# A two-block transformer kernel: norm factors spread by transposition, and wider products in the last up projection

## The chip, the core and the metric

The kernel runs on one core of a Trainium2 chip. The core has five engines that run side by side, each through its own queue in order: TensorE (PE: matrix products, with PEld for the load of the stationary operand), VectorE (DVE), ScalarE (ACT), GpSimd (POOL) and SyncE (SP, which starts the DMAs here). The metric is the time of one execution on the device in microseconds (us).

## What is computed

`reference.py` chains two layers over 256 positions of width 1024, in fp32. Cut to the parts that matter here:

```python
# first block
h = rmsnorm(x, g_mix);  z = h @ w_in            # gated conv branches, then
x = x + (g_a * y_a + g_b * y_b) @ w_o
u = rmsnorm(x, g_ffn) @ w_up                    # 1024 -> 2 x 2816
f = gelu(causal_dwconv(u[:, :D_FF]) + b) * u[:, D_FF:]
x = x + f @ w_down
x = x + sigmoid(rmsnorm(x, g_ple) @ w_ple_gate) * (p @ w_ple)
x = rmsnorm(x, g_final)
# second block
proj = rms_norm(x, attn_pre_g) @ w_in_2         # 8 window heads, 4 differential heads
x = x + rms_norm(mix @ w_out_2, attn_post_g)    # the "post-norm" below
u = rms_norm(x, ffn_pre_g) @ w_up_2             # 1024 -> 2 x 4096
c = causal_dwconv3(u, conv_w) + conv_b
x = x + rms_norm((gelu(c[:, :4096]) * c[:, 4096:]) @ w_down_2, ffn_post_g)
```

## The kernel before

Activations lie feature first: a tile is 128 features by 256 positions. Each fp32 operand of a product is split into a high part in the rounded format fp32r and the remainder, and a product `w x` becomes `wh xh + wh xl + wl xh`. Weights come in 128x128 blocks, eight to a group: SP loads a group (`raw`), ACT casts it to `hi`, DVE (in some stretches POOL) subtracts to get `lo`. An activation's two parts lie next to each other in one tile (`cr`).

There are two ways to run a block. `run` (line 463) issues three products of 256 columns: `wh xh`, `wh xl`, `wl xh`, all into one half of a PSUM bank, so a bank holds two output tiles. `run2` issues, for each group of eight blocks, eight products of 512 columns (`wh` against both parts at once, into a whole bank), then eight of 256 (`wl xh`); the two halves of the bank are added when it is read. So an output tile takes a whole bank. `w_o`, `w_down` and, from tile 4 on, `w_up` use `run2`; `w_up_2` uses `run` throughout.

An RMS norm is applied late where it can be: the products run on `x * g`, and the factor `1/rms` is multiplied in when the bank is read (`evac_pair`). Factors come from `norm_task`: a sum of squares, `s.mean` (products with a column of ones, one output column), `rstd` (DVE adds epsilon, POOL takes the power -0.5), then `spread_mm`, which copies the 2x128 factors over 128 partitions by a product of a broadcast column with the identity. `spread_mm` is called for 13 norms. `normed_task` makes operands that already hold the factor (`hn2` for `w_up`).

All instructions are recorded through `Plan`, whose cost table keeps a clock for each engine. A task is a generator; when it yields a list of tiles, `Plan.spawn` puts it on a heap with the time at which these are expected, and it goes on when TensorE's planned time has reached that. So the plan sets where, among the weight products, a norm's products stand in TensorE's queue. A task that yields "dve" goes on when the plan sees DVE idle.

At the end of attention stands the post-norm: four squares on ACT, sums on DVE, `mean` products, `rstd`, `spread_mm`, and then `x5_task` builds the new x and the operands of `w_up_2`, one of eight at a time. In between, `warm(n)` issues n transposes of the identity into an unused bank. The first four tiles of `w_up_2` then run with k outermost; after them, for each j from 4 to 31, two tiles of `w_up_2` (16 blocks) and, from j = 6 on, eight blocks of `w_down_2`, which accumulate in four banks.

Of the kernel before, what the change touches and what calls it, by code (L numbers as in the profile page):

```python
# [17 lines left out]
P = 128  # L18
T = 256
# [21 lines left out]


QA_PERM = [h * 64 + d for c in range(4) for h in (c, c + 4) for d in range(64)]
LAG2, OLD1, DOWN1, NGAP, PLU, POOL_END2 = 6, 4, 2, 0.9, (30, 8), 1


def _blocks(name, ms, ks):
# [118 lines left out]
    return [(name, i) for i in range(lo // T, hi // T + 1)]  # L166


class Plan:


# [38 lines left out]
    def spawn(self, gen):  # L210
        try:
            y = next(gen)
        except StopIteration:
            return
        if callable(y):
            self.waiting.append((y, gen))
        elif isinstance(y, str):
            self.fill[y].append(gen)
        else:
            self.n += 1  # L220
            at = self.now + y if isinstance(y, (int, float)) else self.at(y) - 0.15
# [116 lines left out]
def block_kernel(ctx: ExitStack, tc: tile.TileContext, w, xT, pT, vec, dist, gpost, out):  # L338
# [43 lines left out]
    def cf():  # L382
        return ap.tile([P, T], F32, tag="c", name=nm("cf"), bufs=NC)
# [27 lines left out]

    names = {}
    EARLY, LAST2 = 4, 4
    WARMA, WARMB = 8, 14
    POOL_END = 4
    POOL_LO, PL1, PL2, LIVE = 8, 0, 0, 4

# [187 lines left out]
    def spread_mm(q, r2):  # L605

        for h in range(2):
            TE.matmul(
                q[:, h * P : (h + 1) * P], lhsT=r2[:, h : h + 1].to_broadcast([P, P]), rhs=ident,
                start=True, stop=True,  # L610
            )

    def norm_task(s, d, box, keep=True, bank=None):

        yield s.done
        yield [s.acc]
        q = Bank()
        s.mean(q, d)
        yield [q.t]
        r = rstd(q[:, :2], 2)  # L620
        yield [r]
        spread_mm(q[:, T:], r)
        if keep:
            yield [q.t]
            o = cf()
            S.copy(o, q[:, T:])
            box[0] = o
            if bank is not None:
# [196 lines left out]
    def ln_task():  # L825
        yield lambda: lastconv[0]
        s = Sum(4, V)
        for c in range(4):
            s.add(acc[c])
        yield [s.acc]  # L830
        q = Bank()
        TE.matmul(q[:, :T], lhsT=ones512, rhs=s.acc, start=True, stop=True)
        yield [q.t]
        sv = Sum(4, V)
        ts = []
        for c in range(4):
            V.tensor_tensor(acc[c], acc[c], q[:, :T], op=ALU.subtract)
            t = cf()
            S.activation(t, acc[c], AF.Square)
            ts.append(t)  # L840
        for t in ts:
            sv.add(t)
        preload(AF.Silu)
        rl = [None]
        plan.spawn(norm_task(sv, 512, rl, False))
        yield lambda: rl[0] is not None
        yield [rl[0]]
        for c in range(4):
# [89 lines left out]
        S.activation(hl[:, 0, :], n, AF.Identity, scale=vec1(g, j))  # L938
        plan.spawn(lo_scaled(n, hl, vec1(g, j), h, j, s))

    def normed_task(r, g, h):

        yield lambda: r[0] is not None
        yield [r[0]]
        for j in range(8):
            t = cf()
            V.scalar_tensor_tensor(t, x[j], vec1(g, j), r[0], op0=ALU.mult, op1=ALU.mult)
            plan.spawn(split_task2(t, h, j))
            yield NGAP
# [191 lines left out]
    def r45_task():  # L1141
        yield lambda: n45[0] == 8
        q = q45
        ms = q[:, :4].rearrange("p (b i) -> p i b", i=2)
        yield [q.t]
        r4 = rstd(ms[:, 0, :], 2)
        yield [r4]
        t = small(2)
        V.tensor_tensor(t, ms[:, 1, :], r4, op=ALU.mult)
        V.tensor_tensor(t, t, r4, op=ALU.mult)  # L1150
        r5 = rstd(t, 2)
        spread_mm(q[:, T:], r4)
# [300 lines left out]
    xt = [[None, None], [None, None]]  # L1453
    gp = []
    og = []
    acc6 = None
    for p in range(4):
        sq = ap.tile([P, 512], F32, tag="pair", name=nm("pT"), bufs=NPAIR)
        S.activation(sq, ob[p].t, AF.Square)
        t = cf()  # L1460
        V.tensor_tensor(t, sq[:, :T], sq[:, T:], op=ALU.add)
        if p in (1, 2):
            V.tensor_tensor(t, t, acc6, op=ALU.add)
        last6, acc6 = acc6, t
    q6 = Bank()
    for n, a in enumerate((last6, acc6)):
        for h in range(2):
            mmul(q6[:, h : h + 1], a[:, h * P : (h + 1) * P], means[DM], q6.first(), n == 1)
    for p in range(4):
        u = pair()  # L1470
        for i in range(2):
# [36 lines left out]

    plan.spawn(x5_task())
    del ob, odst  # L1510
    f, ups = [None] * 32, [0, 0]

    def f2_task(j, q):
        yield lambda: r7[0] is not None
        yield [q.t, r7[0]]
        yield lambda: ups[0] - ups[1] < 4
        u = evac_pair(q, r7[0])
        ups[0] += 1
        del q
# [12 lines left out]
        hl = parts()  # L1532
        S.copy(hl[:, 0, :], c)
        yield [hl]
        V.tensor_tensor(hl[:, 1, :], c, hl[:, 0, :].bitcast(F32), op=ALU.subtract)
        f[j] = hl

    ffn_first("w_up_2", 4, 32, h7, f2_task)
    plan.spawn(xt_task())
    down = [[Bank() for _ in range(2)] for _ in range(2)]  # L1540

    def run_half(tt, k, wh, wl, fp, banks=(0, 1)):
        plan.work(plan.at((wh, wl, fp)))
        a, b = (fp[:, i, tt * P : (tt + 1) * P] for i in range(2))
        for i in banks:
            o = down[tt][i].t
            cs = slice(i * 512, (i + 1) * 512)
            mmul(o, a, wh[:, cs], k == 0, False)
            mmul(o, a, wl[:, cs], False, False)
            mmul(o, b, wh[:, cs], False, k == 31)  # L1550
# [43 lines left out]
        D.dma_start(out=t, in_=gpost[:, i * 512 : (i + 1) * 512])  # L1594
        gp.append(t)
    for j in range(4, 32):
        plan.until(lambda: ups[0] > j - 4)
        q = Bank()
        run(("w_up_2", j), {j: (q, 0), 32 + j: (q, 1)}, h7, 7)
        plan.spawn(f2_task(j, q))  # L1600
        del q
        if j >= LAG2:
            run_down(j - LAG2)
    for k in range(32 - LAG2, 32 - LAST2):
# [68 lines left out]
```

## Time and profile before

| | us |
|---|---|
| median of 3 runs (lowest, highest) | 776.12 (775.79, 776.43) |
| profiled execution | 775.53 |
| its span in the profile | 773.7 |
| busy: PE, DVE, ACT, POOL | 757.9, 627.5, 451.6, 91.0 |

The span is what the profile shows of the execution; some 1.8 us lie around it. PE is busy in 98% of the span. A row of PE gives a start, a length, the product's output and operands, and in brackets the idle time before it and what ended that.

### The profile page before, as it was taken

What the parts mean: (1) busy time and instruction counts of PE and PEld (TensorE: products, weight loads), DVE (VectorE), ACT (ScalarE), POOL (GpSimd) and SP (SyncE); (2) the same over time, 40 slices, a digit from 0 to 9 for tenths busy, and PEclk for the clock granted to TensorE, in tenths of its full rate; (3) what the DMA queues carried; (4) which work ended last, traced back from release to release, by engine and by line L of the source; (5) the groups of instructions that cost most, each with busy time, mean ns of one, the idle gap of its engine ahead of it and who ended that gap; (6) DMA issues with size and microseconds to landing.
All of it is one profiled execution on the core that took longest, in us unless ns stands there. A gap on an engine that the chain in (4) does not pass through costs nothing.

```text
span 773.7 us, 14017 instructions
## 1 busy us (share of the span) xinstructions
PE 757.9 (98%) x5364; PEld 708.6 (92%) x5364; DVE 627.5 (81%) x1149; ACT 451.6 (58%) x797; POOL 91.0 (12%) x75
## 2 busy tenths in 40 slices
PE   7999999999999999999999999999999999999996
PEld 7999999999888888889988899999999999999995
DVE  5699978898988886756879896889978787777883
ACT  7575466566766664545738554757655555555551
POOL 2589200022000000111000010220000000000000
PEclk9999999999999999999999999999999999999999
DMA  8656637454665556555335345354655555555531
GB/s 302 224 183 218 195 135 235 159 178 138 219 199 199 185 180 215 166 201 178 99 94 196 105 149 159 103 191 136 219 193 188 181 182 193 180 191 186 196 110 54
DMA packets 39667, 135.69 MB, mean 175 GB/s; under 512 B 4528, under 2 KB 6320, under 8 KB 39600
## 3 DMA queue, kind: packets, MB, share of 16 engines
q1 hardware_dynamic: 39600, 134.80, 53.0%
q8 instruction: 42, 0.69, 0.4%
q14 instruction: 25, 0.20, 0.1%
HBM read 133.73 MB, written 1.05 MB: 174 GB/s over the span
## 4 chain that ended last, share of the span: by engine, by line
PE 92%; DVE 2%; issue 2%; POOL 1%; DMA 1%; ACT 1%; SPq 0%; POOLq 0%; DVEq 0%; ACTq 0%
PE ps L289 92%; DMA pair<-xT_in 1%; POOL cf L289 1%; DVE cf L289 1%; SPq L289 0%; POOL small L289 0%; DVE lo L289 0%; ACT hi L289 0%; ACT pT L289 0%; ACT cf L289 0%; DVE pT L289 0%; DVE small L289 0%; DVE pair L289 0%; ACT cr L289 0%; POOLq L1668 0%
## 5 line engine op out<-in xcount | busy, mean ns | idle before, releaser
L289 PE MATMUL ps<-cr,hi 128*128 128x256 f32 (+1 forms) x2880 | 568.9, 305 | 4.3 <-ACT hi L289 4.3
L289 PEld LDWEIGHTS ps<-cr,hi 128*128 128x128 f32 x2880 | 462.8, 192 | 23.7 <-ACT hi L289 4.3
L289 PE MATMUL ps<-cr,lo 128*128 128x256 f32 x1704 | 411.3, 283 | 0.3 <-DVE lo L289 0.3
L289 DVE TENSOR_TENSOR lo<-raw,hi 128x1024 fp32r<-128x1024 f32 (+2 forms) x237 | 284.5, 1214 | 40.9 <-ACT hi L289 39.9
L289 PEld LDWEIGHTS ps<-cr,lo 128*128 128x128 f32 x1704 | 301.8, 192 | 8.2 <-DVE lo L289 0.7
L289 ACT CAST hi<-raw 128x1024 fp32r<-128x1024 f32 (+2 forms) x255 | 258.1, 1028 | 36.6 <-PE ps L289 18.3
L289 PE MATMUL ps<-hi,cr 128*128 128x512 f32 (+2 forms) x320 | 98.2, 375 | 0.0
L289 DVE SCALAR_TENSOR_TENSOR cf<-pair,vt,cf 128x254 f32<-128x254 f32 (+2 forms) x144 | 66.4, 481 | 19.8 <-ACT cf L289 17.3
L289 DVE SCALAR_TENSOR_TENSOR cf<-ps,vt,cf 128x255 f32<-128x255 f32 (+30 forms) x172 | 69.2, 458 | 5.4 <-ACT cf L289 4.6
L289 PEld LDWEIGHTS ps<-hi,cr 128*128 128x128 f32 x320 | 58.9, 188 | 10.5 <-issue 0.7
L289 ACT ACTIVATE cf<-pair,vt 128x256 f32<-128x256 f32 x68 | 37.5, 599 | 49.6 <-DVE pair L289 49.6
L289 POOL TENSOR_TENSOR small<-small,mh 128x2 f32<-128x2 f32 (+1 forms) x15 | 14.5, 968 | 407.0 <-DVE small L289 399.0
L289 POOL TENSOR_TENSOR cf<-cf,cf 128x256 f32<-128x256 f32 x28 | 31.1, 1110 | 260.4 <-ACT cf L289 250.0
L289 PE MATMUL ps<-lo,cr 128*128 128x512 f32 (+2 forms) x160 | 60.0, 375 | 0.0
L289 ACT CAST cr<-cf 128x256 fp32r<-128x256 f32 x66 | 26.5, 407 | 55.2 <-DVE cf L289 55.1
L289 POOL TENSOR_TENSOR lo<-raw,hi 128x1024 fp32r<-128x1024 f32 x18 | 42.9, 2416 | 10.0 <-ACT hi L289 8.4
L289 ACT ACTIVATE cf<-cf 128x256 f32<-128x256 f32 x62 | 25.2, 416 | 23.7 <-DVE cf L289 23.6
L289 DVE TENSOR_TENSOR pair<-ps,cf 128x512 f32<-128x512 f32 (+1 forms) x58 | 35.5, 615 | 3.1 <-ACT cf L289 1.9
L289 ACT ACTIVATE cr<-pair,vt 128x256 fp32r<-128x256 f32 x24 | 12.2, 510 | 43.5 <-DVE pair L289 43.5
L289 DVE TENSOR_TENSOR cr<-cf,cr 128x256 fp32r<-128x256 f32 x64 | 26.2, 420 | 11.8 <-ACT cr L289 11.7
L289 PEld LDWEIGHTS ps<-lo,cr 128*128 128x128 f32 x160 | 30.2, 189 | 4.0
L289 ACT COPY cf<-ps 128x256 f32<-128x256 f32 x50 | 18.3, 367 | 23.8 <-PE ps L289 23.7
(104 smaller groups left out, 385.0 us busy)
## 6 DMA issues: line engine op xcount, KB each, us to landing
raw<-w_in SPq DMA_DIRECT2D x244, 512.0 KB, 4.0
raw<-w_in SPq DMA_DIRECT2D x8, 320.0 KB, 2.9
pair<-xT_in SPq DMA_DIRECT2D x8, 128.0 KB, 5.6
out<-pT SPq DMA_DIRECT2D x3, 256.0 KB, 2.1
pair<-gpost_in SPq DMA_DIRECT2D x2, 256.0 KB, 4.9
vt<-vec_in SPq DMA_DIRECT2D x1, 420.5 KB, 6.1
dt<-dist_in SPq DMA_DIRECT2D x1, 384.0 KB, 7.2
raw<-w_in SPq DMA_DIRECT2D x2, 128.0 KB, 2.2
```

Of the source, the lines that this page charges most:

```text
L289: r = f(*args, **kw)
```

## The change

Four things are changed. (1) `spread_mm` uses TensorE's transpose in place of a product with the identity. (2) In the post-norm the last pair's squares are no longer added up on DVE: both halves go to `mean` products of their own (eight such calls in place of four); seven `warm` transposes now stand ahead of the means, and seven in place of fourteen behind the spread. (3) A norm task that yields `Late([...])` goes on 0.6 us later in the plan's time. (4) From j = 15 on, `w_up_2` runs with `run2` on operands `hn7` that already hold the factor; `hn7` is made by `normed_task` in DVE's idle time, and each of the two tiles of a j gets its own bank, read by the new `f2b_task`. The four banks of `w_down_2` are taken when first used. In `w_up` the tile 4 goes from `run2` to `run` (OLD1 from 4 to 5).

```diff
+LATE = 0.6
+OLD2, WAIT2 = 15, 2
-LAG2, OLD1, DOWN1, NGAP, PLU, POOL_END2 = 6, 4, 2, 0.9, (30, 8), 1
+LAG2, OLD1, DOWN1, NGAP, PLU, POOL_END2 = 6, 5, 2, 0.9, (30, 8), 1
...
             at = self.now + y if isinstance(y, (int, float)) else self.at(y) - 0.15
+            if isinstance(y, Late):
+                at += LATE
...
-    WARMA, WARMB = 8, 14
+    WARM0, WARMA, WARMB = 7, 8, 7
...
-            TE.matmul(
-                q[:, h * P : (h + 1) * P], lhsT=r2[:, h : h + 1].to_broadcast([P, P]), rhs=ident,
-                start=True, stop=True,
-            )
+            TE.transpose(q[:, h * P : (h + 1) * P], r2[:, h : h + 1].to_broadcast([P, P]), ident)
...
     def norm_task(s, d, box, keep=True, bank=None):
-        yield [s.acc]
+        yield Late([s.acc])
...
-        yield [r]
+        yield Late([r])
...
         S.activation(sq, ob[p].t, AF.Square)
+        if p == 3:
+            sums6 += [sq[:, :T], sq[:, T:]]
+            break
...
     q6 = Bank()
+    warm(WARM0)
...
+    hn7 = [None] * 8
+    plan.spawn(normed_task(r7, "ffn_pre_g_2", hn7, "dve"))
...
+    def f2b_task(j, qg, qv):
+        cs = []
+        for i, q in enumerate((qg, qv)):
+            yield [q.t]
+            t = cf()
+            S.copy(t, q.half(1))
+            yield [t]
+            if i == 0:
+                u = pair()
+            V.tensor_tensor(u[:, i, :], q.half(0), t, op=ALU.add)
...
+            c = conv3_first(u[:, i, :], "conv_w_2", 64, n, "conv_b_2")
+            yield [c]
+            conv3_rest(c, u[:, i, :], "conv_w_2", 64, n)
...
+        else:
+            plan.until(lambda: ups[0] > j - WAIT2)
+            qs = {j: Bank(), 32 + j: Bank()}
+            run2(("w_up_2", j), qs, hn7, 7)
+            plan.spawn(f2b_task(j, qs[j], qs[32 + j]))
```

`Late` also stands on the sum of the layer norm (`ln_task`) and on the first factor of the two norms between the blocks (`r45_task`); the norms of the attention heads don't have it.

**Three places in the order.** TensorE's queue at the post-norm, from the last product of `w_out_2` to the first of `w_up_2`, before (`mean` and `ident` are constants, `cf` sums of squares, `small` the factors, `cr` an activation, `hi` and `lo` weights):

```order
L289 MATMUL ps_5629<-cr_5887,lo_5805 128x256
L289 MATMUL ps_6004<-mean_95,cf_5997 128x1 x2
L289 MATMUL ps_6004<-mean_95,cf_6002 128x1 x2
L289 MATMUL ps_6025<-ident 128x128 x8
L289 MATMUL ps_6004<-ident,small_6023 128x128 x2
L289 MATMUL ps_6036<-ident 128x128 x14
L289 MATMUL ps_6056<-cr_6054,hi_5858 128x256 x2
```

The same place in the changed kernel (`pT` holds the last squares):

```order
L297 MATMUL ps_5639<-cr_5898,lo_5832 128x256
L297 MATMUL ps_6013<-ident 128x128 x7
L297 MATMUL ps_6012<-mean_95,cf_6003 128x1 x2
L297 MATMUL ps_6012<-mean_95,cf_6008 128x1 x2
L297 MATMUL ps_6012<-mean_95,pT_6010 128x1 x4
L297 MATMUL ps_6045<-ident 128x128 x8
L297 MATMUL ps_6012<-ident,small_6043 128x128 x2
L297 MATMUL ps_6056<-ident 128x128 x7
L297 MATMUL ps_6069<-cr_6067,hi_5864 128x256 x2
```

Seven transposes come ahead of the means, the means are eight calls, and half of the transposes behind the spread are gone. A call of `mean` or of the old spread on fp32 data is two instructions on the chip, a transpose is one.

TensorE's queue between the two blocks of the network, where the factor of the norm `g_final` is spread, before (`gsq` sums the squares with the weights of both norms):

```order
L289 MATMUL ps_4290<-gsq,cf_4701 128x2 x2
L289 MATMUL ps_4621<-cr_4491,hi_4487 128x256 x2
L289 MATMUL ps_4621<-cr_4491,lo_4528 128x256
L289 MATMUL ps_4622<-cr_4491,hi_4487 128x256 x2
L289 MATMUL ps_4622<-cr_4491,lo_4528 128x256
L289 MATMUL ps_4622<-cr_4491,hi_4487 128x256 x2
L289 MATMUL ps_4622<-cr_4491,lo_4528 128x256
L289 MATMUL ps_4290<-ident,small_4710 128x128 x2
```

and in the changed kernel:

```order
L297 MATMUL ps_4301<-gsq,cf_4712 128x2 x2
L297 MATMUL ps_4632<-cr_4502,hi_4498 128x256 x2
L297 MATMUL ps_4632<-cr_4502,lo_4539 128x256
L297 MATMUL ps_4633<-cr_4502,hi_4498 128x256 x2
L297 MATMUL ps_4633<-cr_4502,lo_4539 128x256
L297 MATMUL ps_4633<-cr_4502,hi_4498 128x256 x2
L297 MATMUL ps_4633<-cr_4502,lo_4539 128x256
L297 MATMUL ps_4632<-cr_4581,hi_4534 128x256 x2
L297 MATMUL ps_4632<-cr_4581,lo_4561 128x256
L297 MATMUL ps_4632<-cr_4581,hi_4534 128x256 x2
L297 MATMUL ps_4632<-cr_4581,lo_4561 128x256
L297 MATMUL ps_4301<-ident,small_4721 128x128 x2
```

Five blocks of weight products stand between the sum and the spread, where there were three.

TensorE's queue at the start of j = 15 of `w_up_2`, before:

```order
L289 MATMUL ps_6383<-hi_7320,cr_6954 128x512
L289 MATMUL ps_7469<-cr_6054,hi_7351 128x256 x2
L289 MATMUL ps_7469<-cr_6054,lo_7353 128x256
L289 MATMUL ps_7469<-cr_6062,hi_7351 128x256 x2
L289 MATMUL ps_7469<-cr_6062,lo_7353 128x256
```

and in the changed kernel:

```order
L297 MATMUL ps_6712<-hi_7371,cr_6997 128x512
L297 MATMUL ps_7522<-cr_6386,hi_7404 128x512
L297 MATMUL ps_7522<-cr_6393,hi_7404 128x512
L297 MATMUL ps_7522<-cr_7091,hi_7404 128x512
L297 MATMUL ps_7522<-cr_7100,hi_7404 128x512
L297 MATMUL ps_7522<-cr_7192,hi_7404 128x512
L297 MATMUL ps_7522<-cr_7199,hi_7404 128x512
L297 MATMUL ps_7522<-cr_7293,hi_7404 128x512
L297 MATMUL ps_7522<-cr_7300,hi_7404 128x512
L297 MATMUL ps_7522<-cr_6386,lo_7406 128x256
```

Each block has two products in place of three, over the same number of columns, and the eight `lo` products of a group come behind its eight `hi` products.

## Rows read from the trace of the kernel before

**Rows 1.** The page, chain that ended last: shares of the span by engine.

```profile
PE 92%; DVE 2%; issue 2%; POOL 1%; DMA 1%; ACT 1%; SPq 0%; POOLq 0%; DVEq 0%; ACTq 0%
```

**Rows 2.** Windows: stretch, its length, busy us and instructions by engine, clock, DMA.

```profile
50.00:100.00 50.00, 50.00 (x419) 50.00 (x418) 49.63 (x121) 24.93 (x37) 32.56 (x16) 1.00 0.66 209
515.00:560.00 45.00, 45.00 (x347) 43.53 (x346) 44.12 (x78) 33.71 (x61) 0.00 (x0) 1.00 0.56 185
600.00:750.00 150.00, 150.00 (x1061) 141.32 (x1060) 118.68 (x176) 82.59 (x125) 0.00 (x0) 1.00 0.56 183
```

**Rows 3.** Timeline of PE: start and end of 16 blocks of `w_up_2`.

```profile
606.32 0.40 PE L289 MATMUL ps<-cr,hi 128*128 128x256 f32 x2
...
612.07 0.40 PE L289 MATMUL ps<-hi,cr 128*128 128x512 f32 x1
```

**Rows 4.** Timeline of PE: two starts of groups of `w_up`, 15 groups apart.

```profile
195.06 2.00 PE L289 MATMUL ps<-cr,hi 128*128 128x512 f32 x8
...
236.96 2.00 PE L289 MATMUL ps<-cr,hi 128*128 128x512 f32 x8
```

**Rows 5.** Timeline of PE: a spread and four transposes, each with the row behind it.

```profile
513.59 0.60 PE L289 MATMUL ps<-ident,small 128*128 128x128 f32 x4
513.95 0.48 PE L289 MATMUL ps<-cr,hi 128*128 128x256 f32 x2
...
516.55 0.60 PE L289 MATMUL ps<-ident,pair 128*128 128x128 f32 x4
516.90 0.48 PE L289 MATMUL ps<-cr,hi 128*128 128x256 f32 x2
```

**Rows 6.** Timeline of PE: where a norm's product waited, with idle time and releaser.

```profile
179.94 0.71 PE L289 MATMUL ps<-ident,small 128*128 128x128 f32 x4 [0.43 <-POOL small L289]
388.23 0.71 PE L289 MATMUL ps<-ident,small 128*128 128x128 f32 x4 [0.57 <-DVE small L289]
510.53 0.61 PE L289 MATMUL ps<-mean,cf 128*128 128x1 f32 x4 [0.72 <-POOL cf L289]
```

**Rows 7.** Timelines around the layer norm's sum: PE, then DVE.

```profile
103.70 0.70 PE L289 MATMUL ps<-cf,ones 128*128 128x256 f32 x2 [0.88 <-DVE cf L289]
103.57 1.22 DVE L289 TENSOR_TENSOR lo<-raw,hi 128x1024 fp32r<-128x1024 f32 x1
```

**Rows 8.** Timelines of the post-norm: PE, then DVE; last a window of its clock.

```profile
486.06 1.02 PE L289 MATMUL ps<-mean,cf 128*128 128x1 f32 x8 [1.06 <-DVE cf L289]
486.94 1.16 PE L289 MATMUL ps<-ident 128*128 128x128 f32 x8
488.10 1.22 PE L289 MATMUL ps<-ident,small 128*128 128x128 f32 x4
489.11 2.72 PE L289 MATMUL ps<-ident 128*128 128x128 f32 x14
491.58 0.48 PE L289 MATMUL ps<-cr,hi 128*128 128x256 f32 x2
487.12 0.16 DVE L289 TENSOR_SCALAR small<-ps 128x2 f32<-128x2 f32 x1 [0.87 <-PE ps L289]
489.42 0.42 DVE L289 TENSOR_TENSOR pair<-pair,ps 128x256 f32<-128x256 f32 x1 [2.15 <-PE ps L289]
491.01 0.48 DVE L289 SCALAR_TENSOR_TENSOR cr<-pair,vt,cr 128x256 fp32r<-128x256 f32 x1
487.80:491.20 3.40, 3.40 (x16) 3.10 (x15) 1.71 (x5) 1.33 (x5) 0.24 (x1) 0.50 0.00 0
```

**Rows 9.** Groups of instructions by form: busy us, mean ns, idle before.

```profile
L289 DVE SCALAR_TENSOR_TENSOR cf<-pair,vt,cf 128x256 f32<-128x256 f32 x8 | 3.8, 477 | 1.9 <-ACT cf L289 1.9
L289 DVE TENSOR_TENSOR cr<-cf,cr 128x256 fp32r<-128x256 f32 x64 | 26.2, 420 | 11.8 <-ACT cr L289 11.7
L289 DVE TENSOR_TENSOR pair<-ps,cf 128x512 f32<-128x512 f32 x42 | 28.7, 687 | 2.6 <-ACT cf L289 1.9 <-PE ps L289 0.6
L289 ACT COPY cf<-ps 128x256 f32<-128x256 f32 x50 | 18.3, 367 | 23.8 <-PE ps L289 23.7
```

More of the change, by code (lines that the diff above doesn't have):

```diff
@@ L166, in _cells @@
     return [(name, i) for i in range(lo // T, hi // T + 1)]
+class Late(list):
+    pass
 class Plan:
@@ L829, in ln_task @@
             s.add(acc[c])
-        yield [s.acc]
+        yield Late([s.acc])
         q = Bank()
@@ L939, in res2_task, with normed_task @@
         plan.spawn(lo_scaled(n, hl, vec1(g, j), h, j, s))
-    def normed_task(r, g, h):
+    def normed_task(r, g, h, gap=NGAP):
         yield lambda: r[0] is not None
@@ L948, in normed_task @@
             plan.spawn(split_task2(t, h, j))
-            yield NGAP
+            yield gap
     xnew = [None] * 4
@@ L1146, in r45_task @@
         r4 = rstd(ms[:, 0, :], 2)
-        yield [r4]
+        yield Late([r4])
         t = small(2)
@@ L1455, in block_kernel @@
     og = []
-    acc6 = None
+    sums6 = []
     for p in range(4):
@@ L1459, in block_kernel @@
         S.activation(sq, ob[p].t, AF.Square)
+        if p == 3:
+            sums6 += [sq[:, :T], sq[:, T:]]
+            break
         t = cf()
         V.tensor_tensor(t, sq[:, :T], sq[:, T:], op=ALU.add)
-        if p in (1, 2):
-            V.tensor_tensor(t, t, acc6, op=ALU.add)
-        last6, acc6 = acc6, t
+        if p == 1:
+            V.tensor_tensor(t, t, sums6.pop(), op=ALU.add)
+        sums6.append(t)
     q6 = Bank()
-    for n, a in enumerate((last6, acc6)):
+    warm(WARM0)
+    for n, a in enumerate(sums6):
         for h in range(2):
-            mmul(q6[:, h : h + 1], a[:, h * P : (h + 1) * P], means[DM], q6.first(), n == 1)
+            mmul(q6[:, h : h + 1], a[:, h * P : (h + 1) * P], means[DM], q6.first(), n == 3)
     for p in range(4):
@@ L1536, in f2_task @@
         f[j] = hl
+    def f2b_task(j, qg, qv):
[8 more added lines that the diff above has]
+            V.tensor_tensor(u[:, i, :], q.half(0), t, op=ALU.add)
+            del q
+            if i == 0:
+                del qg
+            else:
+                del qv
+                ups[0] += 1
+            yield [u[:, i, :]]
+            n = 32 * i + j
+            c = conv3_first(u[:, i, :], "conv_w_2", 64, n, "conv_b_2")
+            yield [c]
+            conv3_rest(c, u[:, i, :], "conv_w_2", 64, n)
+            if i == 0:
+                S.activation(c, c, AF.Gelu_apprx_tanh)
+            cs.append(c)
+        ups[1] += 1
+        c, d = cs
+        yield [c, d]
+        V.tensor_tensor(c, c, d, op=ALU.mult)
+        yield [c]
+        hl = parts()
+        S.copy(hl[:, 0, :], c)
+        yield [hl]
+        V.tensor_tensor(hl[:, 1, :], c, hl[:, 0, :].bitcast(F32), op=ALU.subtract)
+        f[j] = hl
     ffn_first("w_up_2", 4, 32, h7, f2_task)
     plan.spawn(xt_task())
-    down = [[Bank() for _ in range(2)] for _ in range(2)]
+    down = [[None, None], [None, None]]
     def run_half(tt, k, wh, wl, fp, banks=(0, 1)):
@@ L1545, in run_half @@
         for i in banks:
+            if down[tt][i] is None:
+                down[tt][i] = Bank()
             o = down[tt][i].t
@@ L1596, in block_kernel @@
     for j in range(4, 32):
[L1597 to L1601, printed above, removed]
+        if j < OLD2:
+            plan.until(lambda: ups[0] > j - 4)
+            q = Bank()
+            run(("w_up_2", j), {j: (q, 0), 32 + j: (q, 1)}, h7, 7)
+            plan.spawn(f2_task(j, q))
+            del q
+        else:
+            plan.until(lambda: ups[0] > j - WAIT2)
+            qs = {j: Bank(), 32 + j: Bank()}
+            run2(("w_up_2", j), qs, hn7, 7)
+            plan.spawn(f2b_task(j, qs[j], qs[32 + j]))
+            del qs
         if j >= LAG2:
```

## The prediction, made before the changed kernel was run

> **What bounds the kernel.** I read the chain of waits first: 92% of the span lies on TensorE [rows 1], so time is won only by fewer or shorter instructions there, or by taking away a wait. Next the windows: TensorE is busy all through 50 to 100, 515 to 560 and 600 to 750, and what differs is DVE, which is full in the first (49.63 of 50), nearly full in the second (44.12 of 45) and has a fifth to spare in the third [rows 2]. So DVE can take more work in the third, hardly in the first two. Last the timeline of TensorE, for the places where it waited [rows 6 to 8].
>
> **Products of 512 and 256 columns.** Sixteen blocks in the old form last from 606.32 to 612.07, 5.75 us or 0.3594 us a block [rows 3]. In the other form 15 groups of eight lie between 195.06 and 236.96, 41.90 us or 0.3492 a block [rows 4]. The saving is 0.0102 us a block. It applies to 17 values of j with 16 blocks each, 272 blocks: 2.77 us. Tile 4 of `w_up` goes the other way: 16 blocks, +0.16.
> What the new form adds lies on DVE and ACT. The operands `hn7` cost DVE eight times 0.477 and 0.420 us [rows 9], 7.2 us, mostly between j = 4 and 10; each j from 15 on replaces one read of 0.687 by two additions of about 0.42, so +0.15, and gives ACT two copies of 0.367. DVE is now busy 118.68 of 150 us [rows 2], 6.8 of each 8.57 us that a j takes; 6.95 still fits in 8.4. The 7.2 us meet a DVE that has 0.9 us to spare up to 560, but TensorE does not read it at once: `f[0]` is used only behind j = 6, and the `lo` groups are made several groups ahead. I take 0 for it and keep 5.9 us as the other end: the 16 instructions' 7.2 less the 0.08 by which each overlaps its neighbour on DVE. Four banks of `w_down_2` being taken later can only help.
>
> **Spreads.** A spread now costs four instructions and 0.36 us (513.59 to 513.95); four transposes cost 0.35, so the two that replace it cost 0.18 [rows 5]. Each of the 13 saves 0.18 where TensorE is the bound. The first (of `g_mix`) lies ahead of a DVE-bound stretch and the post-norm is counted apart, so 11 count: 1.98 us.
>
> **The layer norm's sum.** TensorE waits 0.88 us for DVE at 103.70; since a product's shown length of 0.28 overlaps the next by 0.16, 1.04 us are lost [rows 7]. Before it DVE is full [rows 2], so what TensorE saves earlier is lost there, and what DVE saves is won. In the new order POOL takes one subtraction more of this stretch (19 for 18), and DVE one less: 1.22 us [rows 7], less about 0.1 by which neighbours overlap. The factor of `g_mix` arrives later by about 0.2, as it is queued one block later (0.36) and is 0.18 shorter. Net gain 0.95 (bounds: 0, if POOL's is late; 1.04, the whole wait).
>
> **Norm products put later.** With the 0.16 added, 0.59 us are lost at 179.94, 0.73 at 388.23 and 0.88 at 510.53 [rows 6]. In the new order one block more stands ahead of the first (gain 0.36) and two of the second (0.72 of 0.73). At 510.53 two more blocks stand ahead as well; the wait is for a sum that follows the post-norm, which also moves, so it is counted with that. These blocks are work that must be done anyway; each moved factor only comes later to its readers, which hold banks and don't make TensorE wait in the present trace.
>
> **The post-norm.** Before: TensorE idles 1.06 us to 486.06; eight mean instructions take 0.11 each; DVE adds epsilon at 487.12; the spread starts 0.98 later, takes 1.01 and DVE reads it at 489.42; the first operand's low part is done at 491.01 + 0.48 = 491.49; 14 transposes hold TensorE to 491.58 [rows 8]. From 487.80 to 491.20 the granted clock is 0.50, the lower of its two levels (1.2 GHz), after that idle time and the one-column means; that is why the spread takes 1.01 and not 0.36.
> After: seven transposes from about 484.9 at 0.09 to 0.11 end at 485.6, sixteen means end at 487.4, so epsilon comes 0.5 us later; that the last squares need no addition wins nothing, as TensorE is the late one now. The spread of 0.2 instead of 1.01 gives 0.8 back. DVE reads it 0.3 sooner, at 489.1. The seven transposes behind it end before 490, so the operand's low part at 491.2 decides: with 0.1 for the start of the products, 0.4 won. Bounds: 1.3 won, if the means run beside the last squares at no cost; 2.1 lost, if the clock falls across the products (below). At 510.53 TensorE then arrives 0.4 sooner but has 0.72 us more to do, and the sum's chain is 0.2 sooner: of the wait of 0.88, 0.54 more is won.
>
> The Trainium skill ("TensorE: Matmul & The Clock Gate", Part 4: PE-mode transpose) says that transposes don't count as activity for the clock gate. The trace speaks half against it: the clock rose again at 491.20, after 3.4 us that held the four spread products and most of the 14 transposes [rows 8], and no run here tells these apart. By that rule the change takes the last true products out of the post-norm; what it would cost is the second rival.
>
> **Sum.** 2.77 - 0.16 + 1.98 + 0.95 + 0.36 + 0.72 + 0.40 + 0.54 = 7.6 us. Against the profiled execution's 775.53 (span 773.7 and 1.8 around it) that is 767.9; the median of the runs lies 0.6 above that execution, so 768.5.
>
> **Rivals.**
> 1. *DVE passes its new work on.* For it: 515 to 560 is full [rows 2] and `hn7` falls there. Against: the slack of `f` and of the `lo` groups. If half of 5.9 us reaches TensorE 771.5, if all 774.4.
> 2. *The clock falls over the first products of `w_up_2`.* In the changed kernel nothing but one-column means and transposes stand between the last product of `w_out_2` and the first of `w_up_2`, with 1.1 to 1.7 us idle ahead of the latter. For it: the clock already fell once here [rows 8]. Against: 14 + 8 transposes were enough to bring it back. A stretch as long as that of rows 8, 3.4 us, at half the rate costs 1.7; the lost gain of 0.4 comes on top: 770.6. By the rule of the skill above this is the expected case.
> 3. *The later norm products don't pay.* Their factors are late for the readers and the 0.36, 0.72 and 0.54 come back as waits for banks; the layer norm's 0.95 too, if POOL's extra subtraction is late. 771.1. For it: every moved factor moves its readers' order on DVE; against: no bank wait is seen now.
> 4. *Banks turn over too slowly, and it is slower.* From j = 15 two of the four banks beside `w_down_2` are filled per j, and each is freed by an ACT copy and a DVE addition, one behind the other (0.367 + 0.42), instead of one read of 0.687. If the start of each j waits for these 0.8 us, 16 times, 12.8 are lost: 768.5 + 12.8 = 781. It decides from 0.48 us per j on (7.6 / 16). Against: between the end of a bank and its next use lie eight blocks of `w_down_2`, all 16 of the next j and eight more, over 11 us; `w_up` runs in the same form with no wait that the profile shows.
>
> **How the numbers follow.** The forecast holds 62%, with an own range of 767.2 to 770.0; rival 1 13%, rival 2 12%, rival 3 8%, rival 4 4%, 1% for a change that brings nothing. The low end of the range is the forecast with the upper bounds of the post-norm (0.9 more) and 0.6 for the rest: 767.0. The high end holds rivals 2 and 3 and two thirds of rival 1: 772.6. A difference of 0.2%, 1.55 us, is what a measurement of this kernel can tell from none. Only rival 4 is slower by more than that (4%); the top of rival 1 and the no-change case lie near it or within it (3%); the rest is faster, 93%.
>
> **What would show it.** The product groups of j = 15 to 31: 2.79 us each and no idle ahead of them (step 1; idle with DVE or ACT as the releaser would be rivals 1 or 4). The form `ident,small` halved in count. The waits at the places of 179.94 and 388.23 gone or down to 0.2, that at 510.53 down to 0.3 or less, that at 103.70 near 0.4. In the post-norm, DVE's read of the spread about 4.1 us behind the last product of `w_out_2`, before 4.4; and the granted clock there: below 1 in a window that holds products of `w_up_2` is rival 2. I am wrong if TensorE shows idle time above 1 us in all between j = 4 and 31, or if the post-norm is longer than before.

## The result, and the profile after

The changed kernel takes 768.62 us (median of 4 runs, 768.59 to 769.50); before, run beside it, 775.95 (775.78 to 776.43). The ratio is 0.9905, 95% interval 0.9889 to 0.9921: 7.3 us less, where the prediction had 768.5 us. The profiled execution is the slowest of the four, 769.5 us with a span of 767.7, so the stages read from it add up to 6.0 us and not to 7.3.

To place that difference I compare the times at which TensorE has issued equally many columns of weight products (both kernels issue 1,536,000 of them in all). The numbers are after minus before, in us, at places named by the time of before:

| start, 33 | layer norm done, 116 | 187 | 396 | attention done, 476 | post-norm done, 497 | 520 | end, 763 |
|---|---|---|---|---|---|---|---|
| +0.26 | +0.02 | -0.62 | -1.96 | -1.38 | -1.93 | -2.75 | -6.04 |

Half of it (3.29) is won behind 520, in `w_up_2`; the way from 396 to 476, the attention heads, is the one stretch behind the start that loses (+0.58).

The chain of waits of after, shares of the span by engine (before: [rows 1]): it now runs through DVE for 14%, where it was 2% before, most of it between 33 and 104 and between 392 and 440.

```profile
PE 78%; DVE 14%; issue 3%; POOL 2%; DMA 2%; ACT 1%; SPq 0%; POOLq 0%; DVEq 0%; ACTq 0%
```

Windows of after, columns as in [rows 2]; the second was not looked at before the change, and in the kernel before (last line) DVE is as full there, 19.48 of 20. In the third the clock is whole, TensorE never idles, and DVE has taken the new reads.

```profile
50.00:100.00 50.00, 50.00 (x419) 50.00 (x418) 49.86 (x124) 24.52 (x37) 35.39 (x17) 1.00 0.64 209
400.00:420.00 20.00, 19.36 (x142) 18.52 (x140) 19.38 (x67) 17.70 (x55) 0.00 (x0) 1.00 0.46 147
600.00:750.00 150.00, 150.00 (x793) 129.27 (x792) 119.99 (x194) 93.45 (x158) 0.00 (x0) 1.00 0.56 179
...
400.00:420.00 20.00, 20.00 (x135) 18.48 (x133) 19.48 (x67) 16.29 (x51) 0.00 (x0) 1.00 0.44 146
```

Two groups of `w_up_2` in the new form and the first product behind them, on TensorE (these answer to [rows 3, 4]): 16 blocks from 611.87 to 617.43, 5.56 us or 0.3475 a block, and no idle time in brackets.

```profile
611.87 1.98 PE L297 MATMUL ps<-cr,hi 128*128 128x512 f32 x8
613.68 1.12 PE L297 MATMUL ps<-cr,lo 128*128 128x256 f32 x8
614.64 2.00 PE L297 MATMUL ps<-cr,hi 128*128 128x512 f32 x8
...
617.43 0.40 PE L297 MATMUL ps<-hi,cr 128*128 128x512 f32 x1
```

TensorE at a spread, and at the three places of [rows 6]. The spread holds TensorE for 0.14 us (511.78 to 511.92), where it was 0.36 [rows 5]. A longer wait would stand in brackets behind them: by the end of the product ahead of it TensorE idles 0.07 us at the first, not at all at the second and 0.12 at the third.

```profile
511.78 0.38 PE L297 MATMUL ps<-ident,small 128*128 128x128 f32 x2
511.92 0.49 PE L297 MATMUL ps<-cr,hi 128*128 128x256 f32 x2
...
180.32 0.43 PE L297 MATMUL ps<-ident,small 128*128 128x128 f32 x2
...
387.47 0.43 PE L297 MATMUL ps<-ident,small 128*128 128x128 f32 x2
...
508.72 0.61 PE L297 MATMUL ps<-mean,cf 128*128 128x1 f32 x4
```

The layer norm's sum on TensorE, and an earlier row of DVE (answering to [rows 7]): the wait has not shrunk but grown, 0.88 to 1.18.

```profile
104.61 0.70 PE L297 MATMUL ps<-cf,ones 128*128 128x256 f32 x2 [1.18 <-DVE cf L297]
45.01 0.75 DVE L297 TENSOR_TENSOR cr<-ps,cr 128x256 fp32r<-128x256 f32 x2 [1.01 <-ACT cr L297]
```

The post-norm: TensorE, two rows of DVE, and a window over all of it (answering to [rows 8]). The clock is 1.00 throughout; TensorE waits for the first operand, its high part at 489.10 and its low part at 489.74.

```profile
483.46 0.93 PE L297 MATMUL ps<-ident 128*128 128x128 f32 x7
484.22 0.95 PE L297 MATMUL ps<-mean,cf 128*128 128x1 f32 x8
485.03 1.03 PE L297 MATMUL ps<-mean,pT 128*128 128x1 f32 x8
485.93 1.07 PE L297 MATMUL ps<-ident 128*128 128x128 f32 x8
487.08 0.43 PE L297 MATMUL ps<-ident,small 128*128 128x128 f32 x2
487.35 0.93 PE L297 MATMUL ps<-ident 128*128 128x128 f32 x7
489.10 0.39 PE L297 MATMUL ps<-cr,hi 128*128 128x256 f32 x1 [0.82 <-ACT cr L297]
489.74 0.38 PE L297 MATMUL ps<-cr,hi 128*128 128x256 f32 x1 [0.26 <-DVE cr L297]
486.10 0.16 DVE L297 TENSOR_SCALAR small<-ps 128x2 f32<-128x2 f32 x1 [2.04 <-PE ps L297]
487.62 0.42 DVE L297 TENSOR_TENSOR pair<-pair,ps 128x256 f32<-128x256 f32 x1 [1.36 <-PE ps L297]
483.40:491.00 7.60, 6.44 (x53) 5.77 (x53) 3.92 (x11) 5.61 (x13) 0.69 (x1) 1.00 0.02 7
```

Two waits that before does not have, in the attention heads. The first: TensorE comes 2.9 us sooner than before to the products with `pT`, and waits for copies on ACT that are queued behind a cast of weights, which is itself behind an exponential (`ee`) that waited for DVE. Rows of TensorE, then ACT:

```profile
419.99 1.50 PE L297 MATMUL ps<-pT,vv 128*64 128x512 f32 x3 [0.64 <-ACT pT L297]
418.32 0.20 ACT L297 ACTIVATE ee<-ee 128x2 f32<-128x2 f32 x1 [0.54 <-DVE ee L297]
418.43 1.03 ACT L297 CAST hi<-raw 128x1024 fp32r<-128x1024 f32 x1
419.36 1.55 ACT L297 COPY pT<-ps 128x512 f32<-128x512 f32 x3
```

The second: a spread waits for POOL's power. Rows of TensorE, POOL and DVE of after, then POOL and DVE of before at the same place:

```profile
431.12 0.43 PE L297 MATMUL ps<-ident,small 128*128 128x128 f32 x2 [0.77 <-POOL small L297]
429.46 1.61 POOL L297 TENSOR_TENSOR small<-small,mh 128x2 f32<-128x2 f32 x1 [40.87 <-DVE small L297]
429.22 0.16 DVE L297 TENSOR_SCALAR small<-ps 128x2 f32<-128x2 f32 x1
429.30 1.23 DVE L297 TENSOR_TENSOR lo<-raw,hi 128x1024 fp32r<-128x1024 f32 x1
```

```profile
431.68 0.69 POOL L289 TENSOR_TENSOR small<-small,mh 128x2 f32<-128x2 f32 x1 [42.34 <-DVE small L289]
431.44 0.16 DVE L289 TENSOR_SCALAR small<-ps 128x2 f32<-128x2 f32 x1
431.87 1.22 DVE L289 TENSOR_TENSOR lo<-raw,hi 128x1024 fp32r<-128x1024 f32 x1 [0.27 <-issue]
```

The same power takes 0.69 us where DVE's `lo` begins behind it, and 1.61 where the `lo` begins 0.16 us ahead of it. The Trainium skill ("SBUF — State Buffer", Who interferes with whom) says that a DVE instruction with two SBUF inputs and a GpSimd instruction that reads SBUF exclude each other, the one that starts first going through. For the power this trace agrees: it ends 0.54 us behind the end of the `lo`. For the `lo` it does not: the one that begins 0.19 us behind the start of the power takes 1.22 us, no longer than the other.

### The profile page after: what moved, and what is told of

Same layout as the page of the kernel before. It is cut to its first block, busy times and chain, and to the rows that moved or that the text cites. A ratio compares the mean times of both kernels' runs of the same rounds, so it can differ in the third digit from the quotient of the medians.

```text
span 767.7 us, 13510 instructions
## 1 busy us (share of the span) xinstructions
PE 751.1 (98%) x5090; PEld 691.2 (90%) x5090; DVE 630.2 (82%) x1178; ACT 464.4 (60%) x837; POOL 95.0 (12%) x76
## 3 DMA queue, kind: packets, MB, share of 16 engines
HBM read 133.73 MB, written 1.05 MB: 176 GB/s over the span
## 4 chain that ended last, share of the span: by engine, by line
PE 78%; DVE 14%; issue 3%; POOL 2%; DMA 2%; ACT 1%; SPq 0%; POOLq 0%; DVEq 0%; ACTq 0%
PE ps L297 78%; DVE cf L297 7%; DVE lo L297 2%; DVE pair L297 1%; POOL cf L297 1%; DVE ps L297 1%; DVE nm L297 1%; DMA pair<-xT_in 1%; POOL small L297 1%; DMA raw<-w_in 1%; DVE sc L297 1%; ACT hi L297 1%; DVE cr L297 0%; DVE pn L297 0%; SPq L297 0%
## 5 line engine op out<-in xcount | busy, mean ns | idle before, releaser
L297 PE MATMUL ps<-cr,hi 128*128 128x256 f32 (+1 forms) x2624 | 539.6, 318 | 5.5 <-ACT hi L297 4.4
L297 PEld LDWEIGHTS ps<-cr,hi 128*128 128x128 f32 x2624 | 428.9, 191 | 33.1 <-ACT hi L297 4.6
L297 PE MATMUL ps<-cr,lo 128*128 128x256 f32 x1704 | 374.7, 283 | 0.8 <-DVE lo L297 0.8
L297 PEld LDWEIGHTS ps<-cr,lo 128*128 128x128 f32 x1704 | 287.5, 191 | 11.3 <-DVE lo L297 1.2
L297 DVE SCALAR_TENSOR_TENSOR cf<-pair,vt,cf 128x254 f32<-128x254 f32 (+2 forms) x154 | 72.0, 480 | 13.2 <-ACT cf L297 10.7
L297 DVE SCALAR_TENSOR_TENSOR cf<-ps,vt,cf 128x254 f32<-128x254 f32 (+30 forms) x170 | 68.2, 458 | 8.5 <-ACT cf L297 7.6
L297 ACT CAST cr<-cf 128x256 fp32r<-128x256 f32 x75 | 29.5, 403 | 42.6 <-DVE cf L297 42.5
L297 DVE TENSOR_TENSOR pair<-ps,cf 128x256 f32<-128x256 f32 (+1 forms) x76 | 38.6, 511 | 13.3 <-ACT cf L297 11.3
L297 ACT COPY cf<-ps 128x256 f32<-128x256 f32 x82 | 29.7, 364 | 23.3 <-PE ps L297 23.3
L297 DVE TENSOR_TENSOR cr<-cf,cr 128x256 fp32r<-128x256 f32 x73 | 29.7, 418 | 4.6 <-ACT cr L297 4.3
```

Source lines behind the costliest of these rows:

```text
L297: r = f(*args, **kw)
```

## The experiments

Each was timed beside the kernel before; a ratio below is to that. A table of the stages, as above, stands behind the three sets.

**First set: one part of the change at a time, on the kernel before.**

Products alone (hn7, `OLD2` = 15, `OLD1` = 5, `f2b_task`; spreads, `Late` and post-norm as before; the edit is shown against the changed kernel, and cut):

```diff
-            TE.transpose(q[:, h * P : (h + 1) * P], r2[:, h : h + 1].to_broadcast([P, P]), ident)
+            TE.matmul(q[:, h * P : (h + 1) * P], lhsT=r2[:, h : h + 1].to_broadcast([P, P]), rhs=ident, ...)
-LATE = 0.6
+LATE = 0.0
-    WARM0, WARMA, WARMB = 7, 8, 7
+    WARM0, WARMA, WARMB = 0, 8, 14
```

> The kernel before with part (4) alone: hn7, products of 512 and 256 columns from j = 15 on, OLD1 from 4 to 5. Theory: TensorE is the bound there and the new form saves its time and nothing else. The trace of after shows 8.305 us per j where before had 8.500, so 17 x 0.195 = 3.3 us, less 0.16 for tile 4 of w_up: 772.8 us. Rival (DVE passes hn7 on): the 5.9 us of hn7 reach TensorE by half, 775.8 or more. Step of the prediction: 2.77 - 0.16 = 2.6, that is 773.4.

Measured: 773.23 us against 775.55, ratio 0.9968 (0.9957 to 0.9980). From 520 to the end it wins 3.29 us, as after does; `hn7` makes no wait. It loses 0.95 in the attention, where its instructions and their order are those of before: POOL's power takes 1.61 us there, for 0.69. So it is not shown that this loss is the work of the edit.

Spreads alone (only the `TE.transpose` of the change):

> The kernel before with part (1) alone, spreads by transposition. Prediction: 11 spreads save 0.18 each, and the post-norm a little more (its spread lay under the halved clock, 1.01 us): 1.98 to 2.3, so 773.7 to 774.0 us. Theory of a give-back: the attention heads between 400 and 470 are bound by DVE, ACT and POOL, so the five or six spreads ahead of it (0.9 to 1.1 us) win nothing: gain 1.0 to 1.3, 774.7 to 775.0.

Measured: 774.71, ratio 0.9989 (0.9980 to 0.9998). The time is the one of the give-back theory: TensorE waits 0.62 for `pT` at 421.81 and 0.76 for POOL at 432.94, and the heads as a whole lose 0.61. But it comes to them only 0.17 us ahead of before, so that what they lose is not a lead given back.

`Late` alone (`LATE = 0.6`, `OLD1 = 4`):

> The kernel before with part (3) alone, Late 0.6. Prediction: 0.36 at 179.94, 0.72 at 388.23 and part of 0.88 at 510.53: gain 1.1 to 1.9, 774.0 to 774.9 us. Theory of a give-back: the 1.08 won ahead of the attention is lost there again, and only the last one stays: gain 0.5 to 0.9, 775.1 to 775.5. Layer norm's sum: if it gains 0.95 by POOL's extra subtraction, that comes on top, 773.1 to 774.0, and its wait is near 0.1 to 0.4 in this trace.

Measured: 777.67, ratio 1.0032 (1.0019 to 1.0044): slower, which neither theory had. The gain ahead of the attention is there (layer norm 1.31, and no wait at its sum), and lost at once at tile 4 of `w_up`, whose first products need all of `hn2`. Timeline of TensorE there, a window of the clock, and two rows of TensorE in the heads:

```profile
192.86 0.49 PE L297 MATMUL ps<-cr,hi 128*128 128x512 f32 x1 [0.17 <-DVE cr L297]
195.85 0.79 PE L297 MATMUL ps<-cr,hi 128*128 128x512 f32 x1 [2.49 <-DVE cr L297]
194.66:201.49 6.83, 5.64 (x17) 4.85 (x18) 6.76 (x13) 3.59 (x7) 0.00 (x0) 0.50 0.52 164
...
426.12 1.07 PE L297 MATMUL ps<-pT,vv 128*64 128x512 f32 x2 [0.64 <-ACT pT L297]
437.25 0.60 PE L297 MATMUL ps<-ident,small 128*128 128x128 f32 x3 [0.77 <-POOL small L297]
```

The later factor makes `hn2` late, TensorE idles 2.5 us, and the clock halves for 6.8 us. Both waits of the heads are there too, though TensorE comes to them 4.15 us later than before.

Post-norm alone (old spread, `LATE` = 0):

> The kernel before with part (2) alone: seven transposes ahead of the means, eight mean calls, seven transposes behind; the spread stays a product with the identity. Prediction (clock falls whatever stands there): the means cost 0.5 more and the spread stays at 1.01, so no gain or a loss of 0.3, 775.9 to 776.3 us, with the granted clock at 0.50 for about 3.4 us. Rival: it is the idle time of 1.06 us ahead of the means that lets the clock fall; with transposes there the clock stays at 1.00, the spread takes 0.36, and the post-norm gains 0.3 to 0.6, 775.4 to 775.7.

Measured: 775.73, ratio 1.0003 (0.9994 to 1.0012). The clock stays whole, as the rival said, but of its gain only 0.28 us shows in the stage, and nothing in the time.

```profile
485.20:491.70 6.50, 5.41 (x45) 4.73 (x43) 2.75 (x8) 4.44 (x12) 0.69 (x1) 1.00 0.02 8
```

**Second set.** `Late` with tile 4 moved, on the kernel before (the edit is shown against `Late` alone):

```diff
-LAG2, OLD1, DOWN1, NGAP, PLU, POOL_END2 = 6, 4, 2, 0.9, (30, 8), 1
+LAG2, OLD1, DOWN1, NGAP, PLU, POOL_END2 = 6, 5, 2, 0.9, (30, 8), 1
```

> The kernel before with part (3) and OLD1 = 5, so that tile 4 of w_up runs on the operands without the factor and the first products on hn2 come a tile (5.7 us) later. Theory (OLD1 is the cover of Late): the 2.5 us of idle time at 195.85 and the stretch at half the clock behind it, seen with Late alone, are gone, and what is left of Late shows: the layer norm's wait gone (1.0), 0.4 at 180, 0.7 at 388, less about 1 us lost in the attention heads: 773.5 to 774.8 us. Rival (Late itself costs): the wait only moves to tile 5, and the kernel stays slower than before, over 776.5.

Measured: 773.96 against 775.39, ratio 0.9981 (0.9973 to 0.9990). `OLD1` is the cover of `Late`: no wait at tile 4 or 5. It has won 2.2 by 396 and loses 1.61 of it in the heads (1.56 us of wait at 420.25, 0.77 at 431.38).

A copy behind the epsilon, in the changed kernel:

```diff
         V.tensor_scalar(v, src, EPS, None, op0=ALU.add)
+        V.tensor_copy(cf()[:, :256], src[:, :1].to_broadcast([P, 256]))
         r = small(n)
```

> The changed kernel; behind the DVE instruction that adds epsilon, DVE first copies one PSUM column over 256 columns into a scratch tile (about 0.35 us), 10 to 13 times, before its next instruction. Theory (POOL's power is held up by a DVE subtraction lo that starts just ahead of it): the power takes 0.69 us at all places instead of 1.6 at five of them; the waits at 180.3, 359.6 and 431.1 (0.23, 0.23 and 0.93 us) go or fall below 0.1: 767.0 to 767.8 us. Rival (the power is slow for a reason of POOL's own): it stays at 1.6 at the same places, and the copies cost nothing or up to 0.5 us: 768.6 to 769.2.

Measured: 769.37, ratio 0.9923 (0.9909 to 0.9936): not less than after. The power is 0.69 to 0.72 us at all 13 places, so its cause is shown: what DVE begins ahead of it. But at the other place TensorE now waits 1.74. POOL and DVE, then TensorE and ACT:

```profile
430.05 0.69 POOL L297 TENSOR_TENSOR small<-small,mh 128x2 f32<-128x2 f32 x1 [42.29 <-DVE small L297]
429.88 0.42 DVE L297 COPY cf<-ps 128x256 f32<-128x256 f32 x1
430.24 1.23 DVE L297 TENSOR_TENSOR lo<-raw,hi 128x1024 fp32r<-128x1024 f32 x1
...
420.58 0.64 PE L297 MATMUL ps<-pT,vv 128*64 128x512 f32 x1 [1.74 <-ACT pT L297]
419.00 1.04 ACT L297 CAST hi<-raw 128x1024 fp32r<-128x1024 f32 x1 [1.00 <-DMA raw<-w_in]
```

The cast that stands ahead of the copies waits here for its weights to land. It does so without the copy behind the epsilon too (DVE's sums, below), so it is not shown that this copy made the wait longer.

The new products from j = 12 on (`OLD2 = 12`):

> The changed kernel with OLD2 = 12 in place of 15. Theory (TensorE bound, 0.195 us for each j in the new form): 3 x 0.195 = 0.6 us faster, 768.0 us. Rival: hn7 is complete at 584.6 us in the trace of after and j = 12 begins at about 580, so TensorE waits for the last operands; 1 to 4 us slower than after, 769.6 to 772.6, with idle time on TensorE between 580 and 590 and DVE cr as its releaser.

Measured: 773.31, ratio 0.9979 (0.9970 to 0.9988), 4.7 us above after. The rival is right, and worse than it said, since the clock halves behind the wait (582.05 to 585.46, 0.50):

```profile
581.41 0.90 PE L297 MATMUL ps<-cr,hi 128*128 128x512 f32 x2 [2.96 <-DVE cr L297]
```

No transposes ahead of the means (`WARM0 = 0`):

> The changed kernel with WARM0 = 0: TensorE idles from the last product of w_out_2 (483.4) to the first mean (about 484.2), 0.8 us, and all else is as in after. Theory (idle time ahead of the means lets the clock fall): the granted clock goes to 0.50 behind it for about 3.4 us, the spread and the transposes take twice their time, and the post-norm is 0.3 to 1.0 us longer: 768.9 to 769.6 us. Rival (the transposed spread or the halved number of transposes is what keeps the clock): it stays at 1.00, 768.6 us or 0.1 less. By the Trainium skill (TensorE: Matmul & The Clock Gate, Part 4: PE-mode transpose) transposes don't count for the gate, so that the clock would be the same with or without them.

Measured: 769.86, ratio 0.9933 (0.9921 to 0.9946). The idle time was only 0.26 us, since the sums were ready sooner than I took from after, and still the clock fell, for 6.8 us:

```profile
483.44 1.02 PE L297 MATMUL ps<-mean,cf 128*128 128x1 f32 x8 [0.26 <-DVE cf L297]
486.44:493.26 6.82, 6.67 (x28) 5.97 (x29) 5.78 (x13) 4.76 (x10) 1.29 (x2) 0.50 0.09 10
```

The post-norm stage loses 1.15 where after wins 0.55; 0.4 comes back at the next wait.

**Third set, on the changed kernel.** Lambda early (its lines moved out of `v_task`, unchanged):

```diff
+    def lam_task():
+        yield "dve"
+        ...
+    plan.spawn(lam_task())
     live = [0]
```

> The changed kernel; the scalar lambda of the differential heads (four DVE instructions on constants, one exponential on ACT, three more on DVE) is made in DVE's idle time before the heads begin, and not behind the value projection. In ACT's queue the three copies of transposed probabilities (pT) then stand ahead of the cast hi that stood before them. Theory (TensorE's lead is lost at 420, where its product waits for pT copies that are queued behind a cast, which itself waits for DVE or for its weights): the wait of 0.64 to 1.7 us at 420 goes, and 0.5 to 0.8 us is won: 767.8 to 768.1 us. Rival (DVE as a whole bounds the heads, so the lead is lost at the next place): the wait at 420 goes and reappears between 425 and 450; 768.5 to 769 us.

Measured: 769.78, ratio 0.9933 (0.9920 to 0.9947), above the times of both. In the trace the rival is right: the wait at 420 is gone, and the next one has grown from 0.77 to 1.01.

```profile
431.40 0.43 PE L297 MATMUL ps<-ident,small 128*128 128x128 f32 x2 [1.01 <-POOL small L297]
429.74 1.60 POOL L297 TENSOR_TENSOR small<-small,mh 128x2 f32<-128x2 f32 x1 [41.04 <-DVE small L297]
```

Lambda early and the copy, both:

> The same with the copy behind the epsilon too. Theory: with the place at 420 open, the 0.23 + 0.23 + 0.77 us that the quicker powers gave ahead of and behind it stay won as well: 0.8 to 1.2 us below the kernel with lambda alone, 766.7 to 767.3 us. Rival (DVE bounds the heads; the copies are DVE work): no gain over lambda alone, 767.9 to 768.8 us.

Measured: 768.66, ratio 0.9915 (0.9901 to 0.9928). Both waits are gone in the trace (0.10 left at 429.63), which ends 1.2 us ahead of after's profiled one, 0.2 of it from the start. In the medians it is 1.1 below lambda alone, as the theory had, but not below after; the time is the rival's.

DVE's sums in the post-norm, with 14 transposes ahead (cut):

```diff
-    WARM0, WARMA, WARMB = 7, 8, 7
+    WARM0, WARMA, WARMB = 14, 8, 7
-        if p == 3:
-            sums6 += [sq[:, :T], sq[:, T:]]
-            break
```

> The changed kernel with the post-norm's sums made as before (all of the last pair added on DVE, four mean calls), 14 transposes ahead of the means and 7 behind the spread. The post-norm of the kernel before, where its clock does not fall (before with Late and OLD1 = 5), took 0.63 us less than with the fall; the changed one 0.55 less. Theory (the eight mean calls cost what the last addition saved; only the clock and the shorter spread count): 0.2 to 0.4 us faster than the changed kernel, 768.2 to 768.4 us, epsilon about 0.3 sooner behind the last product of w_out_2. Prediction's view (the eight calls cost 0.5 of TensorE and win nothing) agrees in sign. Rival (DVE's additions are late, by 0.9 behind the last square as in the kernel before): the same time or 0.3 slower.

Measured: 769.03, ratio 0.9921 (0.9908 to 0.9935). The stage wins 0.67 against 0.55, too little to see in the time: the eight mean calls are worth nothing against the addition that they save. Up to the post-norm its instructions and their order are those of after, and yet the heads lose 1.56 in this trace, for 0.58. Rows of TensorE and ACT there:

```profile
420.40 1.07 PE L297 MATMUL ps<-pT,vv 128*64 128x512 f32 x2 [1.61 <-ACT pT L297]
418.81 1.04 ACT L297 CAST hi<-raw 128x1024 fp32r<-128x1024 f32 x1 [0.87 <-DMA raw<-w_in]
```

In this execution the cast ahead of the copies waited for its weights, and no edit stands ahead of it.

All three:

> Lambda early, the copy behind the epsilon, and DVE's sums with 14 transposes ahead, in one kernel. If the three gains are independent (0.6, 1.0, 0.3): 766.7 us. If DVE bounds the heads, only 0.3 to 0.6 remain: 768.0 to 768.3 us.

Measured: 768.15 (768.02 to 768.48), ratio 0.9910 (0.9896 to 0.9923), as expected if DVE bounds the heads. After has 0.9905 (0.9889 to 0.9921), so a better version is not shown, though this one has the earliest end of all traces.

The stages, us against before, one profiled execution each:

| | 33 | 116 | 187 | 396 | 476 | 497 | 520 | end |
|---|---|---|---|---|---|---|---|---|
| products alone | 0.82 | 0.83 | 0.83 | 0.74 | 1.69 | 1.86 | 1.29 | -2.00 |
| spreads alone | 0.77 | 0.65 | 0.37 | -0.17 | 0.44 | 0.11 | 0.03 | 0.03 |
| Late alone | 0.37 | -0.94 | -1.30 | 4.15 | 4.82 | 4.20 | 3.62 | 3.62 |
| post-norm alone | 0.34 | 0.36 | 0.36 | 0.35 | 0.37 | 0.09 | 0.21 | 0.20 |
| Late, tile 4 | -0.44 | -1.73 | -2.09 | -2.66 | -1.05 | -1.68 | -2.26 | -2.26 |
| copy | 0.63 | 0.09 | -0.83 | -2.50 | -1.43 | -1.98 | -2.79 | -6.07 |
| from j = 12 | -0.95 | -1.16 | -1.81 | -3.14 | -2.54 | -3.09 | -3.89 | -2.87 |
| WARM0 = 0 | -0.51 | -0.71 | -1.35 | -2.69 | -1.82 | -0.67 | -1.89 | -5.18 |
| lambda | 0.00 | -0.22 | -0.86 | -2.20 | -1.10 | -1.64 | -2.43 | -5.71 |
| lambda, copy | 0.07 | -0.47 | -1.39 | -3.06 | -2.59 | -3.14 | -3.94 | -7.23 |
| DVE's sums | -0.35 | -0.57 | -1.21 | -2.55 | -0.99 | -1.66 | -2.46 | -5.75 |
| all three | -0.02 | -0.55 | -1.46 | -3.14 | -2.68 | -3.35 | -4.16 | -7.44 |

The first column holds the place and the form of one spread and nothing else of the change; that it goes from -0.95 to +0.82 is how far executions differ, and why a stage is read from the difference of two columns. That difference varies as well. From 396 to 476 after, spreads alone, j = 12, `WARM0` = 0 and DVE's sums have the same instructions in the same order on every engine, and lose 0.58, 0.61, 0.60, 0.87 and 1.56; before, products alone and post-norm alone share another order, and lose 0, 0.95 and 0.02.

## Why the prediction was right, and where it was not

The time was right to 0.1 us, and the mechanism of the largest term; but two terms failed, the layer norm's sum and the spreads in the heads. In the traces these two and the start fall short of the forecast by 2.8 us, the others, most of them too small, give back some 1.2, and 6.0 are left of the 7.6. The medians differ by 7.3 because the profiled execution of after lies 0.9 above its median and that of before 0.4 below its own. That the forecast met the median to 0.1 us is in part luck.

1. *Products of 512 and 256 columns*: 2.77 predicted, 3.29 seen, the same in the products alone. A block takes 0.3475 and not the 0.3492 of [rows 4]: 272 x 0.0119 = 3.2. A whole j took 8.50 us before, where the prediction used 8.57, which changes nothing in it, and takes 8.31 now. No TensorE time was lost to `hn7` or to banks, so rivals 1 and 4 are out; 0 was the right end for `hn7`, though j = 12 shows that it is complete only a few tiles ahead of its use.
2. *Tile 4* was to cost 0.16 and gave 0.09. I had read it as 16 blocks at a dearer price and missed what it is for: it is the condition of `Late`, which without it is 2.1 us slower than nothing.
3. *Spreads*: 0.18 each predicted, 0.22 seen (0.36 to 0.14). But five of the 11 that I counted lie in the attention heads.
4. *The layer norm's sum* failed. Of 0.95 nothing came: the wait is 1.18. POOL did take the 19th `lo` and DVE has 20 for 21, but DVE then idled 1.01 at 45.01 for ACT, and counted from the start column its sum is done 0.65 later than before; the 0.24 that the stage did win is less than its shorter spread alone (0.47 at 109.19, now 0.14). The step that failed is "what DVE saves is won": it holds only while DVE is the last in its chain. Other traces bear this out: in the copy that idle time is 0.64 and the sum 0.35 later; in the spreads alone and in `Late` alone it is not there, and the sum is 0.21 and 0.26 sooner. But even so no more than a quarter shows of the 1.1 that DVE was to save; where the rest went is open. `Late` alone took the wait away mainly because two blocks more stand ahead of the sum there (0.72), where after has one more.
5. *Norm products later*: 0.36 at 179.94 (the wait of 0.43 is 0.07 now), 0.72 at 388.23 (0.7 of the 1.20 there, the rest two spreads). 510.53: 0.54 and a spread predicted (its own terms, 0.72 + 0.2 - 0.4, give 0.52), 0.82 seen, so 0.6. All three as worked out.
6. *The post-norm*: 0.40 predicted, 0.55 seen. DVE's epsilon is 0.4 later behind the last product of `w_out_2` and its read of the spread 0.4 sooner. The low part of the operand decides, as said. Rival 2 did not come. How much of the 0.55 the edits themselves won is open: post-norm alone won 0.28, and `Late` with tile 4, which has none of them, won 0.63 in an execution in which the clock did not fall.
7. *What was missing*: a term for the attention. I counted five spreads there as won, 0.9 us, in windows that I had not read; in the profile of after the heads cost 0.58 more. Two waits stand one behind the other, 0.64 for `pT` and 0.77 for the power. With the first or the second alone taken away the other stayed (1.01 at 431, 1.74 at 420), and the heads lost 1.10 and 1.07. With both gone they lost 0.47, and 0.46 in the kernel with all three: the least of all traces that have the new spreads, though with TensorE further ahead than in after. But the same instructions as in after lost 0.58 to 1.56, so that one trace does not price a wait, and the 1.10 and 1.07 lie inside that. Nor is the loss a lead that is given back: the spreads alone lost as much with 0.17 us of lead as after with 1.96 and j = 12 with 3.14. Shown is the cause of the slow power, and that the saving of five spreads did not appear; why the heads lose time in the new order is open. With both waits gone nothing is lost up to 435 (-3.06 and -3.08), and all of it behind, where idle times of 0.20 at 439.22 and 0.10 at 456.32 are the only ones above 0.06 us, where before has none.

The parts do not add up. Alone they give -2.32, -0.84, -1.43 and +0.18, together -4.4 us for the 7.3 of the whole. In the traces three of them lose time in the heads, 0.95 + 0.61 + 1.61 = 3.2, and the whole loses 0.58 once, which would leave 0.3. But this sets single traces beside medians, and the 0.95 is a loss that the same instructions did not have in two other executions; that the heads explain the gap is not shown.

## What to carry to other kernels

Before summing savings, read the windows of every stage in which they lie: in a stage in which DVE or ACT is full, shorter work on TensorE may not show at all, and two waits in series should be taken away together before either is priced. Price a stage from several executions of the same instructions; here they differed by up to 1 us, which is more than most of the edits were worth. An edit that puts a factor later needs the place where its first reader stands; look for the edit in the diff that moves that reader, and cost the two as one.

## What the runs showed of the chip

- The power on two columns took POOL 0.69 to 0.72 us or 1.60 to 1.67, with one place at 1.2 and one at 0.8; 0.36 us of other DVE work behind the epsilon made all 13 quick. In the 14 traces all 76 slow ones have a DVE subtraction of two SBUF tiles that began 0.09 to 0.16 us ahead of them, and they end 0.54 to 0.57 us behind its end: a `lo` of 1024 columns, at the place with 1.2 one of 640, at the place with 0.8 a `cr` of 256. None of the 106 quick ones has such an instruction ahead of it.
- The clock in the post-norm, one trace a kernel: with 7 or 14 transposes ahead of the means it stayed whole in 8 of 8; without them it fell in 4 of 6. Of these six, "before" and "Late, tile 4" run the same instructions there, with 1.06 us of idle time ahead of the means in both; it fell in one and not in the other, and the stage without the fall is 0.63 us shorter. So a fall in one trace is no property of the kernel. The Trainium skill ("TensorE: Matmul & The Clock Gate", Part 4: PE-mode transpose) says that transposes don't count as activity for the gate. Where they stood ahead of the means, nothing but transposes, one-column means and idle time filled the 5.6 us from 483.46 to 489.10, and the clock stayed at its upper level of 2.4 GHz: this speaks against the rule, without proving the opposite.
- A halved clock behind an idle time adds a price of its own: with `Late` alone the way from 187 to 198 lost 5.9 us, of which 2.7 were idle time.
